# Hybrid decoder layer on one core: token-pass weights rounded two column tiles ahead, and a second instance's token sums cast by halves

## The chip, the cores and the metric

The kernel runs on one core of one Trainium2 chip. A core has a matrix engine (TensorE, PE in the profile, with PEld for its weight loads), a vector engine (VectorE, DVE), a scalar engine (ScalarE, ACT), a general engine (GpSimd, POOL) and a queue engine (SyncE, SP) that issues transfers. Each engine takes its own instructions in a fixed order and waits where an operand is not there yet. The metric is the device time of one execution in microseconds (us); less is better. Every instruction has a line of the kernel in the profile (L1051 is line 1051).

## The reference, cut to what matters

One layer of a hybrid decoder for a prompt of 1024 tokens and 8 single sample tokens, all in 32-bit floats. The 1032 token columns (NT) run through the same weights.

```
h    = rmsnorm(x, norm1_w);  proj = h @ w_in          # 1024 -> 6672 columns
o_a  = gated linear recurrence (8 heads), gated rmsnorm
y    = Mamba-2 mixer (16 heads), gated rmsnorm
x    = x + concat(o_a, y) @ w_out                      # 2048 -> 1024
h    = rmsnorm(x, norm2_w)
gate, val = split(h @ w_up)                            # 1024 -> 2 * 2816
gate = causal_conv(gate, width 3)
x    = x + (silu(gate) * val) @ w_down                 # 2816 -> 1024
y_prompt, y_sample = rmsnorm(x, final_norm_w)
```

The recurrent states and the convolution rows are returned too. The change lies in `concat(o_a, y) @ w_out`, in the second rmsnorm, and in the first two of 22 steps of `h @ w_up`.

## The kernel before, in words

**Precision.** A product of 32-bit values is made from three matmuls on a rounded type (fp32r): each operand is split into a high part (a cast on ACT) and a low part (operand minus high part, on DVE), and PE adds high times high, low times high and high times low. So every weight tile costs an ACT cast, then a DVE subtraction, before PE can use it.

**Jobs.** The first half of the kernel is a list of jobs (`jobs`, L212), each with a load and a run that yields after every matmul. `step` (L255) runs one matmul; `tick` (L239) counts down pieces of other work that `after(n, work)` (L227) put n matmuls ahead, and `spread` (L246) issues a generator piece by piece. PE's order is exactly the written one. On ACT, DVE, POOL and SP a planner orders the instructions by the place at which the program issues them, but by its own cost model it lets a later one pass if the earlier one is not ready; `issue_after(ins)` forbids that an instruction passes `ins`.

**The output projection** is a row of `out_job`s (L1095) over eight column tiles m of 128 columns each:

- a0..a7 and b0..b7: the second and the first 1024 rows of `w_out`, token half 0
- c0..c7: second 1024 rows, token half 1, both quarters of 258 tokens in one job, 48 matmuls
- d00..d07: first 1024 rows, the first quarter of token half 1 only, 24 matmuls each
- d17 down to d10: the same rows, second quarter, 24 matmuls each. The weights of tiles 4 to 7 are kept from the first pass (`wkept`); tiles 3 to 0 are loaded and rounded anew.

A `Weight` (L1034) starts a 512 KB transfer into one of two raw buffers (`ws`); `round` (L1042) casts (L1050) and subtracts (L1051) into a slot pair `wh`, `wl`. The raw buffer is free for the next transfer when the subtraction has ended. Slot pairs come from `wpool` (two) or from `tmp` (two; only tiles 4 and 5 use them). `step` calls `load_ahead` with a depth of 3 jobs and has the next job's weights rounded 1 matmul (24-matmul jobs) or 10 matmuls into the current job. Inside `round` the cast is put behind `mark` (`behind`, L1029): the last square of a finished tile. When a tile's matmuls end, DVE adds the result to x (L1125), SP writes it out (L1135), ACT squares it (L1138, L1141) and POOL adds the square to the row sums (L1142).

**The norm and the token sums.** Tokens go through the up projection in two instances i = 0, 1 (token halves), each of two quarters. `set_norm(i, c)` (L1231) sums the squares over partitions by two matmuls with ones (`n2ms`), and ACT and DVE make the reciprocal root. `set_of(i)` (L1240) scales the tokens (`norm`, L1254) and makes seven operands p1 to p7 (a Strassen-like scheme of seven products in place of eight): p1, p2, p4 are blocks of the tokens themselves, p5, p6, p7, p3 are sums and differences of blocks. `comb` (L1270) makes a sum in two pieces of 516 elements; `put` (L1264, L1265) casts on ACT and subtracts on DVE, for a sum in one piece of 1032. For i = 1, p5 comes from sa = b1 - b2 (DVE), p6 from sa - a1, p7 from sb = a1 - b1 (POOL), p3 from the next sa + a2, one in the place of the other.

**The up projection** (`ups`) runs 22 steps j. A step has 14 products of 12 matmuls: in step 0 all seven of instance 0 and then all seven of instance 1, in the order p1, p2, p4, p5, p6, p7, p3; later steps alternate the instances. `up_split(j, n)` (L1342) casts two weight parts of a step (L1351) and subtracts (L1352). The parts of step 1 are issued in step 0 after the sixth, tenth and fourteenth product. The results of p2, p4, p5, p6 go to four PSUM banks (`ub`), those of p1, p7, p3 to three others (`ua`); DVE and ACT empty them (L1374 to L1409), and `up_close` ends a step with the convolution and SiLU.

**Driving order around the change**: after d07, `set_norm(1, 0)` is put 20 matmuls ahead and ten pieces of `set_of(1)` (those that need only the first quarter) one per 10 matmuls from the 40th; `up_split(0, n)` follow in d13, d11, d10; in step 0, `set_norm(1, 1)` stands after 44 matmuls, and the other pieces of `set_of(1)` follow from the 46th, one per matmul.

Of the kernel before, what the change touches and what calls it, by code (L numbers as in the profile page):

```python
# [9 lines left out]
F32 = mybir.dt.float32  # L10
# [3 lines left out]
ALU = mybir.AluOpType  # L14
# [37 lines left out]
def hybrid_layer(  # L52
# [156 lines left out]

    jobs, loaded, done, later, ahead = [], {}, set(), [], {}  # L212
    at = [0, None]

    def load_ahead(i, n):
# [11 lines left out]
    def after(n, work):  # L227

        item = [n, work]
        later.append(item)  # L230
        return item
# [23 lines left out]
    def step(last):  # L255
        tick()
        if at[1] is None:
            name, load, run = jobs[at[0]]
            nxt = jobs[at[0] + 1][0] if at[0] + 1 < len(jobs) else None
            load_ahead(at[0], 3 if nxt in ahead or name in ahead else 2)  # L260
            if nxt in ahead:
                early, n = ahead[nxt]
                after(n, lambda part=loaded[at[0] + 1]: early(part))
            at[1] = run(loaded[at[0]]) if load is not None else run()
        if next(at[1], None) is None:
            done.add(jobs[at[0]][0])
            at[0] += 1
            at[1] = None
            if last not in done:
                step(last)  # L270
# [821 lines left out]

    wkept, summed = {}, [None, set()]

    def out_job(name, r0, hf, m, cols=(0, 1), begin=None, keep=False):  # L1095
        first, last = r0 == 8, r0 == 0

        def load():
            w = wkept.pop(m, None) or Weight(r0, m)
            if keep:  # L1100
                wkept[m] = w
            return w, residual_load(m, hf) if first else None

        def early(loads):
            loads[0].round(tmp if keep and m in (4, 5) else wpool)

        def run(loads):
            w, res = loads
            early(loads)
            if begin is not None:  # L1110
                begin()
            hi, lo = mixes[r0, hf]
            if first:
                if m % 2 == 0:
                    xpair[hf][m // 2] = tl("big", "x1")[:, :NT].rearrange("p (i t) -> p i t", i=2)
                xh[hf][m] = xpair[hf][m // 2][:, m % 2, :]
            for c in cols:
                cs, ts_ = slice(c * QW, (c + 1) * QW), slice((2 * hf + c) * QW, (2 * hf + c + 1) * QW)
                ps = psmm.tile([P, 512], F32, tag="mm", name=nm("mm"))[:, :QW]
                yield from steps(w.parts, 0, P, hi, lo, cs, ps)  # L1120
                x_ = xh[hf][m][:, cs]
                if first:
                    mark[0] = A.copy(x_, ps)
                else:
                    V.tensor_tensor(x_, x_, ps, op=ALU.add)  # L1125
                    final(m, x_, ts_)
                yield True
            if first:
                spread(residual(xh[hf][m], hf, *res), 8)
        job(name, load, run)  # L1130
        ahead[name] = early, 10 if len(cols) == 2 else 1

    def final(m, x_, ts_):

# [60 lines left out]
    for m in range(KT):  # L1195
        out_job(f"b{m}", 0, 0, m, begin={0: open_b}.get(m))
    for m in range(KT):
        out_job(f"c{m}", 8, 1, m, begin={0: open_c}.get(m))
    for m in range(KT):
        out_job(f"d0{m}", 0, 1, m, (0,), {0: lambda: split_rest(0, 1)}.get(m), m > 3)  # L1200
    for m in reversed(range(KT)):
        out_job(f"d1{m}", 0, 1, m, (1,))

    with tc.manual_schedule(engines={mybir.EngineType.PE}):
        finish("x3")
# [29 lines left out]
        mm(ps[:, :QW], ones, rst[:, cs])  # L1235
        rstd_of(rst[:, cs], tl("us", "nt"), ps[:, :QW], DM)

    usets = [{}, {}]

    def set_of(i):  # L1240

        ts_ = slice(2 * i * QW, 2 * (i + 1) * QW)
        xp = [t.rearrange("p i (c t) -> p i c t", c=2) for t in xpair[i]]

        def block(h1, c):
            return [xp[2 * h1 + q][:, :, c, :] for q in range(2)]

        a1, b1, a2, b2 = block(0, 0), block(0, 1), block(1, 0), block(1, 1)

        def norm(h1, cols=slice(0, MID)):  # L1250
            rs = rst[:, ts_][:, cols]
            for m in range(4 * h1, 4 * h1 + 4):
                x_ = xh[i][m][:, cols]
                V.scalar_tensor_tensor(x_, x_, col("n2", m), rs, op0=ALU.mult, op1=ALU.mult)  # L1254
                yield

        def put(name, src, tag):
            hi, lo = tl(tag, "uh", F32R), tl(tag, "ul", F32R)
            hq, lq = quads(hi[:, :NT]), quads(lo[:, :NT])
            usets[i][name] = hq, lq  # L1260
            n = 4 // len(src)
            for q, t in enumerate(src):
                rows = slice(q * n, (q + 1) * n)
                A.copy(hq[:, rows], t)  # L1264
                V.tensor_tensor(lq[:, rows], t, hq[:, rows].bitcast(F32), op=ALU.subtract)  # L1265
                yield

        def comb(t, eng, x_, y_, op):
            for q in range(2):
                eng.tensor_tensor(t[:, 2 * q:2 * q + 2], x_[q], y_[q], op=op)  # L1270
                yield

        def two(t):
            return [t[:, 0:2], t[:, 2:4]]

        c0, c1 = slice(0, QW), slice(QW, MID)
        if i == 0:
            yield from norm(0)
            yield from norm(1)
            yield from put("p2", a2, "big")  # L1280
            yield from put("p4", b2, "e")
        else:
            yield from norm(1, c0)
            yield from put("p2", a2, "big")
            yield from norm(0, c0)
            yield from put("p1", a1, "hT")
            yield from norm(1, c1)
            yield from put("p4", b2, "hT")
            yield from norm(0, c1)
        sa, sb = (quads(tl("x5", "sm")[:, :NT]) for _ in range(2))  # L1290
        yield from comb(sa, V, b1, b2, ALU.subtract)
        yield from comb(sb, G, a1, b1, ALU.subtract)
        if i == 0:
            while "c7" not in done:
                yield
            yield from put("p1", a1, "hT")
        yield from put("p5", [sa], "hT")
        yield from comb(sa, V, two(sa), a1, ALU.subtract)
        yield from put("p6", [sa], "hT")
        yield from put("p7", [sb], "big" if i else "hT")  # L1300
        yield from comb(sa, V, two(sa), a2, ALU.add)
        yield from put("p3", [sa], "big")

# [38 lines left out]
    def up_split(j, n):  # L1342
# [5 lines left out]
        lo = pool.tile([P, KT * P], F32R, tag="wl", bufs=2, name=nm("wl"))  # L1348
        for i, name in enumerate(order[2 * n:2 * n + 2]):
            cs = slice(i * 512, (i + 1) * 512)  # L1350
            A.copy(hi[:, cs], sums[name])  # L1351
            V.tensor_tensor(lo[:, cs], sums[name], hi[:, cs].bitcast(F32), op=ALU.subtract)  # L1352
            ops_[name] = [t[:, cs].rearrange("p (k m) -> p k m", m=P) for t in (hi, lo)]

# [88 lines left out]
    with tc.manual_schedule(engines={mybir.EngineType.PE}):  # L1443
# [21 lines left out]
        up_split(0, 3)  # L1465
        for _ in early:
            pass
        after(44, lambda: set_norm(1, 1))
        after(46, lambda: spread(second, 1))
        for _ in ups(0, [(name, i) for i in range(2) for name in FIRST]):  # L1470
            tick()
        for j in range(1, FT):
# [124 lines left out]
```

## Time and profile before

| | |
|---|---|
| median of 3 runs | 1792.68 us (1789.44 to 1794.56) |
| profiled execution | 1790.33 us, span 1788.6 us, granted TensorE clock 0.995 |
| PE busy | 1742.4 us, 97% of the span |
| PEld busy | 1684.7 us, 94% |
| DVE busy | 1111.1 us, 62% |
| ACT busy | 797.0 us, 45% |
| POOL busy | 398.2 us, 22% |
| DMA | 105 GB/s mean |

The times in the profile's views count from the start of the span. In a row of the chain of waits the first number is the start, the second the length, both in us, and "x48" is the number of instructions. In a timeline row the same two numbers lead, and the idle time before the row stands in brackets with what ended it. In a table of windows each engine has its busy time and, in brackets, the number of its instructions; PEclk is the granted share of the matrix engine's full clock.

### The profile page before, as it was taken

To read this page: it belongs to the slowest core of one execution; us is meant where nothing else is said; L and a number is where in the kernel's file an instruction comes from. 1 tells how busy PE (TensorE), PEld (TensorE's weight loads), DVE (VectorE), ACT (ScalarE), POOL (GpSimd) and SP (SyncE) were. 2 spreads that over 40 slices of the span, in tenths; PEclk is the share of its full clock that TensorE was granted. 3 is DMA by queue.
4 is the path that set the end of the run, shared out by engine and by line. 5 is a ranking of instruction groups with operands and counts; after the bars stand their busy time and mean duration, and the time that the engine had idled before them with its cause. 6 is when DMAs were issued, how large, how long until landed. Compare 5 with 4: busy or idle time off the path is not lost.

```text
span 1788.6 us, 38536 instructions
## 1 busy us (share of the span) xinstructions
PE 1742.4 (97%) x16223; PEld 1684.7 (94%) x16223; DVE 1111.1 (62%) x1946; ACT 797.0 (45%) x1410; POOL 398.2 (22%) x411
## 2 busy tenths in 40 slices
PE   7999899999999999999999998999999999999998
PEld 7998798999999999999999898999999999999997
DVE  4657967566555554556657668666666666545545
ACT  6477688454544444354344444333433344111114
POOL 1103331110110110111011134454445542000002
PEclk9999999999999999999999998999999999999999
DMA  5135634553222221224466341222222225422212
GB/s 154 36 99 154 171 101 136 170 156 99 72 77 63 73 84 43 81 79 133 144 201 190 113 118 56 87 72 72 84 95 72 72 77 209 143 86 94 96 60 96
DMA packets 240547, 188.66 MB, mean 105 GB/s; under 512 B 13356, under 2 KB 213590, under 8 KB 240358
## 3 DMA queue, kind: packets, MB, share of 16 engines
q1 hardware_dynamic: 240086, 186.11, 34.2%
q8 instruction: 127, 2.08, 0.5%
q14 instruction: 46, 0.38, 0.1%
q0 software_dynamic: 288, 0.10, 0.0%
HBM read 147.84 MB, written 38.52 MB: 104 GB/s over the span
## 4 chain that ended last, share of the span: by engine, by line
PE 46%; DVE 3%; ACT 1%; DMA 1%; issue 0%; DVEq 0%; POOL 0%; ACTq 0%
PE ub L94 14%; PE dn L94 13%; PE ua L94 10%; PE mm L94 7%; DMA ws<-in_w_out_dram 1%; DVE ul L1265 1%; DVE x L1254 0%; DVE wl L1051 0%; DVE sm L1270 0%; PE fin L1552 0%; PE xtp L809 0%; DVE wl L1352 0%; ACT ot L1554 0%; ACT uh L1264 0%; PE l L1491 0%
## 5 line engine op out<-in xcount | busy, mean ns | idle before, releaser
L94 PE MATMUL mm<-hh,wh 128*128 128x344 f32 x1248 | 406.2, 326 | 1.2 <-ACT sz L691 1.2
L94 PE MATMUL mm<-hl,wh 128*128 128x344 f32 x1248 | 403.9, 324 | 0.0
L94 PE MATMUL mm<-hh,wl 128*128 128x344 f32 x1248 | 402.5, 323 | 0.0
L94 PEld LDWEIGHTS mm<-hh,wh 128*128 128x128 f32 x1248 | 234.5, 188 | 4.5 <-ACT sz L691 1.5
L94 PEld LDWEIGHTS mm<-hl,wh 128*128 128x128 f32 x1248 | 234.6, 188 | 2.5 <-issue 0.9
L94 PEld LDWEIGHTS mm<-hh,wl 128*128 128x128 f32 x1248 | 234.8, 188 | 2.2 <-issue 1.0
L94 PE MATMUL ub<-uh,wh 128*128 128x258 f32 x704 | 200.4, 285 | 2.8 <-ACT uh L1264 2.8
L94 PE MATMUL ub<-ul,wh 128*128 128x258 f32 x704 | 200.6, 285 | 2.3 <-DVE ul L1265 2.3
L94 PE MATMUL ub<-uh,wl 128*128 128x258 f32 x704 | 200.0, 284 | 0.0
L94 PE MATMUL mm<-mx,wh 128*128 128x258 f32 x1024 | 191.2, 286 | 2.4 <-DVE mx L1067 1.3
L94 PE MATMUL dn<-ah,wh 128*128 128x256 f32 (+1 forms) x640 | 181.1, 283 | 1.2 <-DVE x L1527 1.2
L94 PE MATMUL dn<-ah,wl 128*128 128x256 f32 (+1 forms) x640 | 180.4, 282 | 0.1
L94 PE MATMUL dn<-al,wh 128*128 128x256 f32 (+1 forms) x640 | 180.3, 282 | 0.0
L189 ACT CAST wh<-ws 128x1024 fp32r<-128x1024 f32 x72 | 75.4, 1048 | 206.7 <-PE dn L94 135.8
L94 PEld LDWEIGHTS mm<-mx,wh 128*128 128x128 f32 x1024 | 158.5, 189 | 3.9 <-DVE mx L1067 1.8
L94 PE MATMUL mm<-mx,wl 128*128 128x258 f32 x512 | 145.9, 285 | 3.9 <-DVE wl L1051 3.8
L94 PE MATMUL ua<-ul,wh 128*128 128x258 f32 x528 | 149.4, 283 | 0.0
L94 PE MATMUL ua<-uh,wh 128*128 128x258 f32 x528 | 149.3, 283 | 0.0
L94 PE MATMUL ua<-uh,wl 128*128 128x258 f32 x528 | 149.2, 283 | 0.0
L94 PEld LDWEIGHTS ub<-uh,wh 128*128 128x128 f32 x704 | 133.8, 190 | 3.4 <-ACT uh L1264 3.3
L94 PEld LDWEIGHTS ub<-ul,wh 128*128 128x128 f32 x704 | 134.2, 191 | 2.8 <-DVE ul L1265 2.8
L94 PEld LDWEIGHTS ub<-uh,wl 128*128 128x128 f32 x704 | 134.3, 191 | 0.0
(332 smaller groups left out, 3739.1 us busy)
## 6 DMA issues: line engine op xcount, KB each, us to landing
ws<-in_w_in_dram SPq DMA_DIRECT2D x52, 512.0 KB
ws<-in_w_up_dram SPq DMA_DIRECT2D x44, 512.0 KB
ws<-in_w_out_dram SPq DMA_DIRECT2D x36, 512.0 KB
act_d<-val SPq DMA_DIRECT2D x22, 516.0 KB
al<-act_d SPq DMA_DIRECT2D x22, 516.0 KB
ws<-in_w_down_dram SPq DMA_DIRECT2D x22, 512.0 KB
mx<-mix_d SPq DMA_DIRECT2D x32, 258.0 KB
csb<-cs_d SPq DMA_DIRECT2D x32, 256.0 KB
```

The source lines that it names most:

```text
L94: PE.matmul(out, lhsT, rhs, start=start, stop=stop)
L189: A.copy(wh[:, :n], ws[:, :n])
L1265: V.tensor_tensor(lq[:, rows], t, hq[:, rows].bitcast(F32), op=ALU.subtract)
```

## The change

Three edits, all in order and place of work; no matmul is added or removed.

1. The weights of a d job are rounded two jobs ahead instead of one (`lead`), with four slot pairs (`pool`: tiles 0, 1, 4, 5 in `tmp`, 2, 3, 6, 7 in `wpool`; the reloaded tiles 3 to 0 in `wpool`). d00 is rounded in c6, d01 in c7. d11 and d10 keep a lead of one. Jobs are loaded deeper ahead (`depth`: 4 from c7 on, up to 6 at d17).
2. In step 0 `set_norm(1, 1)` stands after 22 matmuls, and the rest of `set_of(1)` starts at the 24th. In `set_of(1)` POOL's sb is issued first, and p5, p6 and p3 are made by `comb_put`: each half is added and cast at once, and the two halves' subtractions follow.
3. The casts of step 1's weight parts are put behind the last cast of `comb_put` (`setmark`).

```diff
-            nxt = jobs[at[0] + 1][0] if at[0] + 1 < len(jobs) else None
-            load_ahead(at[0], 3 if nxt in ahead or name in ahead else 2)
-            if nxt in ahead:
-                early, n = ahead[nxt]
-                after(n, lambda part=loaded[at[0] + 1]: early(part))
+            load_ahead(at[0], depths.get(at[0], 3 if at[0] in at_jobs else 2))
+            for i, (j, early) in enumerate(at_jobs.get(at[0], ())):
+                after((1 if name[0] == "d" else 10) + 12 * i, lambda part=loaded[j], early=early: early(part))
...
-            loads[0].round(tmp if keep and m in (4, 5) else wpool)
+            loads[0].round(tmp if pool == "t" else wpool)
...
-        ahead[name] = early, 10 if len(cols) == 2 else 1
+        at_jobs.setdefault(len(jobs) - 1 - lead, []).append((len(jobs) - 1, early))
+        depths[len(jobs) - 1] = depth
...
-        out_job(f"c{m}", 8, 1, m, begin={0: open_c}.get(m))
+        out_job(f"c{m}", 8, 1, m, begin={0: open_c}.get(m), depth=3 if m < 7 else 4)
...
-        out_job(f"d0{m}", 0, 1, m, (0,), {0: lambda: split_rest(0, 1)}.get(m), m > 3)
+        out_job(f"d0{m}", 0, 1, m, (0,), {0: lambda: split_rest(0, 1)}.get(m), m > 3, "ttwwttww"[m], 2, 4)
...
-        out_job(f"d1{m}", 0, 1, m, (1,))
+        out_job(f"d1{m}", 0, 1, m, (1,), pool="wwwwttww"[m], lead=2 if m > 1 else 1, depth=(2, 3, 3, 4, 4, 4, 5, 6)[m])
...
+        def comb_put(name, tag, t, x_, y_, op):
+            hi, lo = tl(tag, "uh", F32R), tl(tag, "ul", F32R)
+            hq, lq = quads(hi[:, :NT]), quads(lo[:, :NT])
+            usets[i][name] = hq, lq
+            half_ = [slice(0, 2), slice(2, 4)]
+            for q, rows in enumerate(half_):
+                V.tensor_tensor(t[:, rows], x_[q], y_[q], op=op)
+                setmark[0] = A.copy(hq[:, rows], t[:, rows])
+                yield
+            for rows in half_:
+                V.tensor_tensor(lq[:, rows], t[:, rows], hq[:, rows].bitcast(F32), op=ALU.subtract)
+            yield
...
+        if i:
+            yield from comb(sb, G, a1, b1, ALU.subtract)
+            yield from comb_put("p5", "hT", sa, b1, b2, ALU.subtract)
+            yield from comb_put("p6", "hT", sa, two(sa), a1, ALU.subtract)
+            yield from put("p7", [sb], "big")
+            yield from comb_put("p3", "big", sa, two(sa), a2, ALU.add)
+            return
...
-            A.copy(hi[:, cs], sums[name])
+            if j == 1:
+                with tc.issue_after(setmark[0].ins):
+                    A.copy(hi[:, cs], sums[name])
+            else:
+                A.copy(hi[:, cs], sums[name])
...
-        after(44, lambda: set_norm(1, 1))
-        after(46, lambda: spread(second, 1))
+        after(22, lambda: set_norm(1, 1))
+        after(24, lambda: spread(second, 1))
```

More of the change, by code (lines that the diff above doesn't have):

```diff
@@ L208, in hybrid_layer @@
     chunks = [slice(c * CH, (c + 1) * CH) for c in range(NCH)]
-    jobs, loaded, done, later, ahead = [], {}, set(), [], {}
+    jobs, loaded, done, later, at_jobs, depths = [], {}, set(), [], {}, {}
     at = [0, None]
@@ L1093, in hybrid_layer, with out_job @@
     wkept, summed = {}, [None, set()]
-    def out_job(name, r0, hf, m, cols=(0, 1), begin=None, keep=False):
+    def out_job(name, r0, hf, m, cols=(0, 1), begin=None, keep=False, pool="w", lead=1, depth=3):
         first, last = r0 == 8, r0 == 0
@@ L1236, in set_norm @@
         rstd_of(rst[:, cs], tl("us", "nt"), ps[:, :QW], DM)
-    usets = [{}, {}]
+    usets, setmark = [{}, {}], [None]
     def set_of(i):
@@ L1290, in set_of @@
         sa, sb = (quads(tl("x5", "sm")[:, :NT]) for _ in range(2))
+        if i:
[5 more added lines that the diff above has]
+            return
         yield from comb(sa, V, b1, b2, ALU.subtract)
         yield from comb(sb, G, a1, b1, ALU.subtract)
[L1293 to L1296, printed above, removed]
+        while "c7" not in done:
+            yield
+        yield from put("p1", a1, "hT")
         yield from put("p5", [sa], "hT")
@@ L1299, in set_of @@
         yield from put("p6", [sa], "hT")
-        yield from put("p7", [sb], "big" if i else "hT")
+        yield from put("p7", [sb], "hT")
         yield from comb(sa, V, two(sa), a2, ALU.add)
```

## The prediction

> **What bounds the kernel now.** I read the page's busy times first, then the waits of PE around the change, the chain of waits there, and last the timelines and groups of ACT, DVE, POOL and SP. The page:
>
> ```profile
> PE 1742.4 (97%) x16223; PEld 1684.7 (94%) x16223; DVE 1111.1 (62%) x1946; ACT 797.0 (45%) x1410; POOL 398.2 (22%) x411
> ```
>
> PE sets the time. An edit of order can only win back time in which PE stands still or runs slowly. Waits of PE from 1000 to 1095 us:
>
> ```profile
> PE mm L94 <- DVE wl L1051: 3.8, 5, 1.4
> PE ub L94 <- ACT uh L1264: 2.8, 2, 1.7
> PE ub L94 <- DVE ul L1265: 2.3, 2, 1.4
> PE mm L94 <- ACT wh L1050: 0.9, 2, 0.7
> ```
>
> Both places of the change are here: the d jobs wait for rounded weights (3.8 + 0.9 us), step 0 for token sums (2.8 + 2.3 us). Waits are not the whole loss, so I count it from the chain of waits:
>
> ```profile
> 994.23 5.97 PE mm L94 x48
> 1000.20 0.44 PE xtp L809 x4
> ...
> 1019.19 5.65 DMA ws<-in_w_out_dram
> ...
> 1027.19 4.13 DMA ws<-in_w_out_dram
> ...
> 1061.88 1.43 PE ua L94 x12
> 1063.31 3.85 PE ub L94 x32
> 1067.16 0.45 PE n2ms L94 x2
> ...
> 1088.25 6.32 PE ua L94 x48
> 1094.57 5.77 PE ub L94 x48
> ```
>
> **d jobs.** An unhindered 258-column matmul takes 5.97/48 = 0.124 us, a tile of 24 takes 2.99. From 994.23 (start of c6) to 1061.88 (end of d10) lie 67.65 us. They hold 2 x 48 matmuls of c6 and c7 and 16 x 24 of the d jobs, 480 x 0.1244 = 59.7, the transposes after c6 and c7 (0.44 and a small one, 0.6 each) and `n2ms` of 0.45: 61.4. So 6.2 us are lost, none of it in c6. **Step 0.** From 1061.88 to 1094.57 lie 32.69 us with 14 x 12 matmuls of step 0 and 24 of step 1: 192 x 0.120 (5.77/48) + 0.45 = 23.5. Lost: 9.2 us, of which 5.1 are waits. The windows show where most of the rest went, and what DVE does meanwhile:
>
> ```profile
> 1068.10:1089.70 21.60, 16.50 (x105) 15.49 (x105) 21.29 (x33) 8.37 (x14) 6.12 (x5) 0.76 0.00 1
> 1076.00:1079.20 3.20, 1.10 (x7) 0.68 (x6) 3.03 (x5) 1.89 (x3) 1.61 (x3) 1.00 0.00 0
> 1079.20:1089.40 10.20, 7.20 (x30) 6.61 (x31) 10.20 (x14) 4.84 (x8) 1.53 (x1) 0.50 0.00 1
> ```
>
> The columns are stretch, length, then busy time of PE, PEld, DVE, ACT, POOL, and the granted clock. PE was busy for 1.10 of 3.20 us, and for the next 10.2 us its clock was 0.50: the waits cost some 4 us more in a slow clock. And DVE is busy for 21.29 of 21.60 us: here it is DVE, not PE, that sets the pace. Recoverable in all: 6.2 + 9.2 = 15.4 us.
>
> **Edit 1, weights two tiles ahead.** It moves one cast (1.03 to 1.06 us on ACT) and one subtraction per tile ahead by a tile; it adds none, and the count of transfers stays (eight for the first pass, four for the second). The subtractions before, of d01 to d07:
>
> ```profile
> L1051 DVE TENSOR_TENSOR wl<-ws,wh x7: 1211/1225/1727, 1008.2 to 1032.5; 128x1024 fp32r<-128x1024 f32 x7
> ```
>
> That is one per 24.3/6 = 4.1 us where PE could take one per 2.99. If the lead only shifts each of these times to the next tile, the time now kept for d01 serves d02, and so on. Unhindered, d0m starts at 994.23 + 2 x (5.97 + 0.6) + 2.99 m, that is 1007.4 + 2.99 m. The rows that decide:
>
> ```profile
> 1014.18 1.22 DVE L1051 TENSOR_TENSOR wl<-ws,wh 128x1024 fp32r<-128x1024 f32 x1
> ...
> 1025.94 1.23 DVE L1051 TENSOR_TENSOR wl<-ws,wh 128x1024 fp32r<-128x1024 f32 x1 [3.27 <-ACT wh L1050]
> 1027.09 0.41 DVE L1125 TENSOR_TENSOR x<-x,mm 128x258 f32<-128x258 f32 x1
> 1028.92 1.23 DVE L1051 TENSOR_TENSOR wl<-ws,wh 128x1024 fp32r<-128x1024 f32 x1 [1.42 <-ACT wh L1050]
> ```
>
> The one that ends at 1015.4 (d02 now, then d03) is 1.0 us early for d03 at 1016.4; the one that ends at 1027.2 (then d06) is 1.9 late for 1025.3; the one at 1030.2 (then d07) is 1.9 late for 1028.3, the same lateness and not a further one. So at fixed times 1.9 us would be left of what d0 loses. The times are not fixed: a cast waits behind the square of an earlier tile, which waits for DVE's addition (L1125, queued behind the subtraction above), and PE will end that tile sooner. Against that stands the raw buffer: cast 1.05, subtraction 1.23 and transfer 4.13 to 5.65 us (chain) make 6.4 to 7.9 us per two tiles where PE takes 5.98, so 0.2 to 1.0 us are lost per tile once the lead is used up. I take 1.2 left in d0 (0 to 3), and 0.5 in d1, whose last two tiles keep a lead of one. **Gain 4.5 us, from 2.5 to 5.7.** Cast and subtraction of d00 and d01 now fall into c6 and c7, where PE runs its 48 matmuls in 5.97 us without a wait; without that cover they would cost a 1.2 us subtraction each. What SP must pass is a transfer issued one job sooner that waits for its buffer; behind it stand only the write-outs of x, for which no engine waits soon.
>
> **Edit 2, step 0.** `n2ms` moves from 44 matmuls in to 22: 22 x 0.120 = 2.65 us sooner, and everything that hangs on it (root, norms, sums) with it. It needs the last row sum on POOL:
>
> ```profile
> 1063.29 0.64 POOL L1142 TENSOR_TENSOR n2r<-n2r,n2sq 128x258 f32<-128x258 f32 x1 [2.09 <-ACT n2sq L1141]
> ```
>
> That ends 2.05 us after PE's step 0 began; the new place is at 2.65, so 0.6 us of room; if DVE is late there, all of PE waits for it, by some tenths. The sums of DVE from 1068 to 1090, by group:
>
> ```profile
> L1270 DVE TENSOR_TENSOR sm<-sm,x 128x516 f32<-128x516 f32 x4 | 2.6, 685 | 0.0
> L1270 DVE TENSOR_TENSOR sm<-x,x 128x516 f32<-128x516 f32 x2 | 2.2, 1138 | 0.0
> ```
>
> A subtraction of a half works on 516 elements like these pieces: some 0.66 us as they follow each other (2.6/4), two 1.3, a whole one 1.23 (row below): +0.1 for each of p5, p6, p3, together 0.3 us, an estimate. The first two sums cost 1138 ns a piece against 685 for the later four; POOL runs its own two pieces of sb in that stretch:
>
> ```profile
> 1075.23 1.49 POOL L1270 TENSOR_TENSOR sm<-x 128x516 f32<-128x516 f32 x1 [0.36 <-DVE x L1254]
> ```
>
> The change puts sb's issue first, so this collision stays, at 0.9 us for the two pieces, and I take no gain from it. The Trainium skill (SBUF — State Buffer, Who interferes with whom) says that a DVE instruction with two SBUF inputs and a GpSimd instruction that reads SBUF exclude each other, and whoever issues second blocks fully. By that rule POOL going first would cost DVE up to the whole 1.49 us per piece and the sum would be some 2 us worse; the trace shows 0.45 a piece, and I go by it.
>
> **Edit 3, step 1's weights behind the sums.** The same stretch for the low weight parts alone (PE and PEld on matmuls that use them, then DVE), and the end of the last token sum:
>
> ```profile
> 1068.10:1089.70 21.60, 11.02 (x35) 7.97 (x35) 3.18 (x4) 0.76 0.00 1
> ```
>
> ```profile
> 1088.46 1.22 DVE L1265 TENSOR_TENSOR ul<-sm,uh 128x1032 fp32r<-128x1032 f32 x1
> ```
>
> Four subtractions, 3.2 us of DVE, leave the stretch ahead of that sum. So p3's operand, complete at 1089.7 (27.8 us into step 0), is complete 2.65 + 3.2 - 0.3 = 5.5 us sooner, 22.3 us in. PE would reach p3 of instance 1 after 156 matmuls, 156 x 0.120 + 0.45 = 19.2 us in. **3.1 us of the 9.2 stay lost, gain 6.1 us**, if no wait is long enough to slow the clock; 0 is left if DVE's emptying of PSUM falls into gaps, 6.5 if the clock slows (by what stays of the 4 us above): 2.7 to 9.2. The postponed weights are then late next: their cast and subtraction (0.6 + 0.7 us) for step 1's p1 come right behind p3's operand, while PE works 12 matmuls on p3 (1.44 us): no wait, and 1.3 us for each part if that cover is gone.
>
> The Trainium skill (TensorE: Matmul & The Clock Gate, HAM oscillation) puts the drop of the clock at idle gaps of over about 3.4 us. Here the longest wait was 1.70 us and the clock still fell, so the trace disagrees if the rule is read as one gap, and agrees if it means a window that is mostly idle. By the single-gap reading no wait left here could slow the clock, and the sum would keep its 6.1 us for certain.
>
> **Sum.** 4.5 + 6.1 = 10.6 us from the profiled execution's 1790.33: 1779.7. That execution is 2.35 us under the median of the runs, 1792.68, so I expect a median of **1782.0 us**.
>
> **Rivals.**
>
> *Emptied too late (B).* Products p2, p4, p5, p6 share four PSUM banks. The addition that empties p6 of instance 0 (L1378) ran between the sums of p5 and their subtraction, in a gap that the whole cast on ACT left:
>
> ```profile
> 1077.20 0.41 DVE L1378 TENSOR_TENSOR us<-us,ub 128x258 f32<-128x258 f32 x1
> ```
>
> Cast by halves leaves hardly a gap, and the sums are now listed 22 matmuls further ahead of this addition. If it falls behind p3's operand, p5 of instance 1 starts about 21 us in and not at 14.9: 6 us of standstill, then a clock of 0.50 for 10.2 us, 5.1 more. 11.1 us lost against 9.2 before, so the sum is 4.5 - 1.9 = 2.6 us: 1790.1. Against it: the cast ends a moment after DVE's second sum, so a small gap remains.
>
> *No gain in the d jobs (C).* DVE stays packed with `set_of(0)`'s sums behind c7 and the raw buffers stay two, so rounding runs at 4.1 us per tile and the lead is used up at once: only the 6.1 us of step 0 remain: 1786.6.
>
> *Second step starved, slower (D).* The postponed subtractions meet the end of step 0 on DVE, and the planner lets later work pass, as here, where a weight part issued later (L1352) went before the d13 subtraction:
>
> ```profile
> 1047.01 1.28 DVE L1352 TENSOR_TENSOR wl<-ws,wh 128x512 fp32r<-128x512 f32 x2
> 1048.22 1.21 DVE L1051 TENSOR_TENSOR wl<-ws,wh 128x1024 fp32r<-128x1024 f32 x1
> ...
> 1094.75 2.65 DVE L358 SCALAR_TENSOR_TENSOR fcv<-fext,vcol,fcv 128x1048 f32<-128x1048 f32 x2
> ...
> 1099.96 2.21 DVE L1425 TENSOR_TENSOR val<-val,fext 128x1032 f32<-128x1032 f32 x1 [1.90 <-ACT fext L1424]
> ```
>
> If the six additions of instance 1 (6 x 0.41 = 2.5 us), the convolution (2.65), the 2.6 us until the product starts (SiLU on ACT, 1097.4 to 1099.96) and the product (2.21) come before step 1's first subtraction, it ends 10.0 + 0.7 us after 22.3, and PE, ready at 23.7, stands for 9 us; with 5.1 for the clock 14 us, which eats 10.6 and 3.4 more: 1796. It turns slower once that wait with its slow clock passes 10.6 us. Against it: the parts are issued before the convolution.
>
> *It does not do what it says (E).* The planner ends in the same order on DVE, which is full either way: 1792.
>
> **How the numbers follow.** Forecast 0.62, B 0.15, C 0.12, D 0.06, E 0.05. The forecast's own range is 1777.8 to 1787.5 (gains of 14.9 to 5.2 by the bounds above). Down to 1776 and up to 1790.5 it takes in C and most of B. A run-to-run spread of 0.3% (5.4 us) is what can be told from no change, so faster means under 1787.3: 0.60 of the forecast, 0.07 of C, 0.03 of B, 0.70. Slower: D and a little of B and E, 0.08. Same: 0.22.
>
> **What would show it.** In the profile of the changed kernel: PE's waits for L1051 and L1050 at 1 to 2 us and not 4.7; `n2ms` 2.65 us into step 0; DVE's L1352 of step 1 behind p3's last L1265; PE's waits for `ub` at 3 us, and no stretch of half clock near 1075. Wrong: a wait of PE for L1378 (B), for L1352 in step 1 (D), or unchanged waits for L1051 (C).

## The result and the profile after

| | before | after |
|---|---|---|
| median | 1794.56 us (7 runs, 1789.44 to 1796.49) | 1788.01 us (7 runs, 1784.51 to 1789.63) |
| profiled execution | 1790.33 us, span 1788.6 | 1789.03 us, span 1787.3 |
| the same kernels timed again | 1793.77 us (15 runs) | 1785.60 us (7 runs) |

The ratio after to before is 0.9966 with an interval of 0.9952 to 0.9981, and 0.9954 (0.9940 to 0.9969) the second time. The kernel is faster by 0.34 to 0.46%, 6.6 and 8.2 us, where 0.6% (10.6 us) was forecast. The first timing stays above the 1787.3 us under which the forecast called it faster.

The two profiled executions differ by 1.3 us only, and that would mislead: in the profile of before, c6 starts at 994.23 us, in that of after at 998.24, after work that the change does not touch: up to there PE, DVE, ACT and POOL run the same instructions in the same order in both. So I compare the two stretches of the prediction. **D** runs from c6 to step 0, **U** from step 0 to the first p6 product of step 1. Chain of waits of after:

```profile
998.24 5.97 PE mm L94 x48
...
1019.45 5.90 DMA ws<-in_w_out_dram
...
1062.02 1.45 PE ua L94 x12
...
1091.18 1.71 PE ua L94 x12
1092.88 5.78 PE ub L94 x48
```

D is 1062.02 - 998.24 = 63.78 us (67.65 before), U is 1092.88 - 1062.02 = 30.86 us (32.69 before). The change gained 3.9 us in the d jobs, where 4.5 were forecast, and 1.8 us in step 0, where 6.1 were. In the second profile of after (from 998.57 to 1062.11 and to 1092.29) they are 63.54 and 30.18: 4.1 and 2.5 us. The miss lies in step 0.

The waits of PE from 1000 to 1100 us, after:

```profile
PE ub L94 <- DVE fext L1424: 1.6, 1, 1.6
PE mm L94 <- DVE wl L1049: 1.5, 2, 0.8
PE mm L94 <- ACT wh L1048: 0.9, 2, 0.6
PE ub L94 <- DVE ul L1285: 0.9, 2, 0.7
PE ub L94 <- DVE us L1400: 0.5, 1, 0.5
PE ua L94 <- ACT us L1396: 0.5, 1, 0.5
```

L1049 and L1048 are the rounding of the d jobs (L1051 and L1050 before): 2.4 us in place of 4.7. L1285 is a token remainder. New are L1424 and L1400, for which PE waits 2.1 us: they are the emptyings of the PSUM banks of p4 and p6 by DVE. L1396 is an emptying by ACT. The windows of after (columns as in the prediction) say what came behind:

```profile
1077.86:1081.27 3.41, 1.75 (x12) 1.57 (x13) 3.41 (x8) 2.15 (x4) 1.10 (x2) 1.00 0.01 2
1081.27:1088.10 6.83, 6.13 (x28) 5.83 (x28) 6.83 (x11) 4.44 (x10) 1.65 (x1) 0.50 0.00 0
```

PE was busy 1.75 of 3.41 us, and its clock then was 0.50 for 6.83 us (10.24 before). The last place to read is what moved next to what. First POOL and DVE of before, around the root of the second norm, then the same of after:

```profile
1063.88 1.29 POOL L1332 TENSOR_TENSOR wt<-ws 128x512 f32<-128x512 f32 x1
...
1067.74 1.29 POOL L1332 TENSOR_TENSOR wt<-wt,ws 128x512 f32<-128x512 f32 x1
```

```profile
1068.14 0.43 DVE L666 SCALAR_TENSOR_TENSOR nt<-n2ms,n2r 128x258 f32<-128x258 f32 x1 [2.85 <-ACT n2r L665]
1068.60 0.72 DVE L667 SCALAR_TENSOR_TENSOR nt<-nt,n2r 128x258 f32<-128x258 f32 x1
1069.35 0.43 DVE L668 SCALAR_TENSOR_TENSOR n2r<-nt,n2r 128x258 f32<-128x258 f32 x1
1069.81 1.69 DVE L1254 SCALAR_TENSOR_TENSOR x<-x,vcol,n2r 128x258 f32<-128x258 f32 x4
```

```profile
1064.16 1.28 POOL L1350 TENSOR_TENSOR wt<-ws 128x512 f32<-128x512 f32 x1
1065.52 1.30 POOL L1350 TENSOR_TENSOR wt<-wt,ws 128x512 f32<-128x512 f32 x1
1066.77 1.48 POOL L1350 TENSOR_TENSOR wt<-ws,ws 128x512 f32<-128x512 f32 x1
1068.21 1.47 POOL L1350 TENSOR_TENSOR wt<-wt,ws 128x512 f32<-128x512 f32 x1
```

```profile
1065.78 0.42 DVE L664 SCALAR_TENSOR_TENSOR nt<-n2ms,n2r 128x258 f32<-128x258 f32 x1
1066.24 0.86 DVE L665 SCALAR_TENSOR_TENSOR nt<-nt,n2r 128x258 f32<-128x258 f32 x1
1067.14 1.40 DVE L666 SCALAR_TENSOR_TENSOR n2r<-nt,n2r 128x258 f32<-128x258 f32 x1
1068.57 2.59 DVE L1253 SCALAR_TENSOR_TENSOR x<-x,vcol,n2r 128x258 f32<-128x258 f32 x4
...
1076.86 0.41 DVE L1400 TENSOR_TENSOR us<-us,ub 128x258 f32<-128x258 f32 x1
...
1080.56 0.41 DVE L1424 TENSOR_TENSOR fext<-us,ub 128x258 f32<-128x258 f32 x1
```

POOL makes four sums of step 1's weights (`up_sums`). Before, they ran from 1063.88 to 1069.03 us, and for 2.85 of these 5.15 us DVE stood idle ahead of the root. The change moved the root into them: the last two operations of the root and the first four norms took 0.86 + 1.40 + 2.59 = 4.85 us and not 0.72 + 0.43 + 1.69 = 2.84. And the emptying of p6 (L1400) and p4 (L1424) of instance 0 stands between the token sums on DVE: p6 was complete 7.8 us into step 0 (1069.7) and p7, which p4's emptying needs, at 9.3 (1071.1), so they are emptied 7 to 9 us late.

### The profile page after: what moved, and what is told of

It is laid out like the page before. It is cut to its first block, busy times and chain, and to the rows that moved or that the text cites. A ratio compares the mean times of both kernels' runs of the same rounds, so it can differ in the third digit from the quotient of the medians.

```text
span 1787.3 us, 38542 instructions
## 1 busy us (share of the span) xinstructions
PE 1742.0 (97%) x16223; PEld 1685.8 (94%) x16223; DVE 1112.5 (62%) x1949; ACT 797.4 (45%) x1413; POOL 397.8 (22%) x411
## 4 chain that ended last, share of the span: by engine, by line
PE 45%; DVE 3%; ACT 1%; DMA 1%; issue 0%; DVEq 0%; POOL 0%; ACTq 0%
PE ub L94 14%; PE dn L94 13%; PE ua L94 10%; PE mm L94 7%; DMA ws<-in_w_out_dram 1%; DVE x L1253 1%; DVE wl L1049 0%; DVE ul L1264 0%; PE fin L1574 0%; PE xtp L807 0%; ACT ot L1576 0%; ACT uh L1263 0%; ACT wh L1048 0%; DVE ul L1285 0%; DVE sm L1281 0%
```

## The experiments

All marks of all kernels, one profile each, are in the table. **R** is the time from step 0's first matmul to the end of p3's last remainder of instance 1 (in after 1061.86 to 1086.23; the matmul's own record starts 0.16 us ahead of its piece of the chain). R marks how far DVE's queue has come; it is not itself what PE waits for in after, where p3's first matmul of instance 1 starts at 1087.35, 1.1 us behind R. "Waits" are PE's waits within U, "rest" is U - 23.5 (PE's unhindered work by the prediction) - waits; "half clock" is the time at 0.50 within U. Medians are given where a kernel was timed more than once (e3 and e4 took 1791.08 and 1790.60 us, one time each). All diffs are against after.

| kernel | D | R | U | waits | rest | half clock | median, ratio to before |
|---|---|---|---|---|---|---|---|
| before | 67.65 | 27.97 | 32.69 | 5.10 | 4.09 | 10.24 | |
| e1_weights | 63.17 | 28.05 | 33.23 | 5.18 | 4.55 | 10.24 | 1790.41, 0.9973 (0.9960 to 0.9985) |
| e2_step0 | 67.45 | 24.02 | 29.77 | 3.75 | 2.52 | 3.41 | 1790.42, 0.9976 (0.9965 to 0.9987) |
| e3_no_behind | 63.41 | 24.66 | 30.37 | 4.08 | 2.79 | 3.41 | |
| e4_norm44 | 63.60 | 25.30 | 31.67 | 3.82 | 4.35 | 6.83 | |
| after | 63.78 | 24.37 | 30.86 | 3.45 | 3.91 | 6.83 | 1788.01, 0.9966 (0.9952 to 0.9981) |
| after_again | 63.54 | 24.32 | 30.18 | 4.04 | 2.64 | 3.41 | 1785.60, 0.9954 (0.9940 to 0.9969) |
| e7_sums_late | 63.57 | 26.06 | 31.35 | 4.86 | 2.99 | 3.41 | 1790.15, 0.9976 (0.9963 to 0.9989) |
| e8_sb_dve | 63.92 | 24.05 | 29.94 | 3.75 | 2.69 | 3.41 | 1789.11, 0.9970 (0.9957 to 0.9983) |
| e10_emptied | 63.31 | 26.11 | 30.78 | 3.48 | 3.80 | 6.83 | 1788.31, 0.9971 (0.9957 to 0.9985) |
| e11_emptied_sums | 63.50 | 29.47 | 33.79 | 7.00 | 3.29 | 6.83 | 1790.88, 0.9982 (0.9973 to 0.9992) |
| e12_sums_last | 63.59 | 22.04 | 27.89 | 3.64 | 0.75 | 0 | 1786.80, 0.9957 (0.9940 to 0.9974) |
| e13_sums_dve | 63.53 | 22.04 | 29.12 | 4.86 | 0.76 | 0 | 1788.12, 0.9967 (0.9954 to 0.9980) |
| e14_three_dve | 63.25 | 22.60 | 28.00 | 3.76 | 0.74 | 0 | 1786.57, 0.9952 (0.9935 to 0.9970) |

D and R repeat to 0.3 us between the two profiles of after. Among kernels that share the part they spread a little more: D from 63.17 to 63.92 in all with edit 1, R from 24.02 to 24.37 in e2 and the two profiles of after, whose step 0 is the same. The rest is 0.75 us without half clock, 2.5 to 3.0 with 3.41 us of it, 3.3 to 4.35 with 6.83, 4.1 to 4.55 with 10.24: a slow clock costs 1.8 to 3.8 us here, and 3.41 against 6.83 us of it is a difference between two runs of one kernel. Medians spread by some 2 us (after alone 1788.01 and 1785.60), so the marks, not the medians, tell these kernels apart.

**Edit 1 alone** (the d jobs' weights two tiles ahead; step 0 as before).

```diff
...
-            yield from comb_put("p5", "hT", sa, b1, b2, ALU.subtract)
...
-                with tc.issue_after(setmark[0].ins):
...
-        after(22, lambda: set_norm(1, 1))
-        after(24, lambda: spread(second, 1))
+        after(44, lambda: set_norm(1, 1))
+        after(46, lambda: spread(second, 1))
```

> The changed kernel with step 0 as before (n2ms after 44 matmuls, whole casts, no cast put behind): only the weights two tiles ahead are left. Measures: D, from the first matmul of c6 to the first of step 0 (67.65 us before, 63.78 in the changed kernel, 61.4 unhindered), and U, from there to the first p6 product of step 1 (32.69 before, 30.86 changed, 23.5 unhindered). Theory 1 (the two parts add up, and the lead won 3.9 us by itself): D 63.8, U 32.7, some 4 us under the kernel before, ratio 0.998. Rival (the two parts disturb each other: DVE work that the lead moves falls into step 0): U over 33.5 or D under 63. Rival C of the prediction (no gain from the lead): D 67.

D fell by 4.48 us, U stayed (33.23, with waits of 5.18). The waits of PE, e1:

```profile
PE ub L94 <- ACT uh L1263: 2.9, 2, 1.8
PE ub L94 <- DVE ul L1264: 2.3, 2, 1.4
PE mm L94 <- DVE wl L1049: 1.5, 2, 0.8
```

The d jobs' part is edit 1's and of the forecast's size; the waits of step 0 are those of before.

**Edits 2 and 3 alone.**

```diff
...
-        out_job(f"d0{m}", 0, 1, m, (0,), {0: lambda: split_rest(0, 1)}.get(m), m > 3, "ttwwttww"[m], 2, 4)
+        out_job(f"d0{m}", 0, 1, m, (0,), {0: lambda: split_rest(0, 1)}.get(m), m > 3, "wwwwttww"[m])
...
-        out_job(f"d1{m}", 0, 1, m, (1,), pool="wwwwttww"[m], lead=2 if m > 1 else 1, depth=(2, 3, 3, 4, 4, 4, 5, 6)[m])
+        out_job(f"d1{m}", 0, 1, m, (1,), pool="wwwwttww"[m])
```

> The changed kernel with the weights of the d jobs rounded one tile ahead in the old slots: only the edits of step 0 are left. Theory 1 (the parts add up, and the edits of step 0 win only 1.8 us because DVE's root and norms now run beside POOL's sums for step 1 and because PE waits for a PSUM bank): D 67.6, U 30.9, 2 us under the kernel before, ratio 0.999. Rival (the lead disturbs step 0; alone its edits win what was forecast): U 26.6, 6 us under.

D is that of before (67.45), U 29.77 and R 24.02: step 0 alone gains 2.9 us, not the 1.8 expected nor the 6 of the rival, with the same wait for L1424 (1.6 us) as after. Alone the two parts gain 4.5 and 2.9 us by the marks, 7.4 in sum; together they gained 5.7 and 6.6 in the two profiles of after. D's spread and the half clock (3.41 us here, 6.83 and 3.41 there) are as large as that difference, so a small hindrance is neither shown nor excluded.

**After without edit 3, and after with the norm at its old place** (44 and 46 in place of 22 and 24).

```diff
-            if j == 1:
-                with tc.issue_after(setmark[0].ins):
-                    A.copy(hi[:, cs], sums[name])
-            else:
-                A.copy(hi[:, cs], sums[name])
+            A.copy(hi[:, cs], sums[name])
```

> The changed kernel without the third edit: step 1's weight casts are not put behind the last token sum. As forecast, this edit takes four subtractions, 3.2 us of DVE, out of the way of the last sum: U 34, D unchanged at 63.8. Rival (postponing costs at the start of step 1 what it wins before): U 30.9 or less.

> The changed kernel with n2ms and the rest of the second token set back at 44 and 46 matmuls. If moving it up won 2.65 us as forecast: U 33.5. Theory 1 (the root and the norms now run beside POOL's four sums for step 1 and take 2 us longer for it: root and first four norms 1.28 + 0.86 + 1.40 + 2.59 us in the place of 1.6 + 1.7): U 31.4, half a us more than the changed kernel's 30.86.

Without edit 3, U is 30.37 and not 34, and R is 24.66 against 24.37 and 24.32: the edit is worth some 0.3 us, no more than the spread of R, and not 3.2. With edit 2 in place only one of step 1's four weight subtractions (L1370) still went ahead of p3's last remainder (L1285), as DVE's timeline without edit 3 shows:

```profile
1086.72 0.68 DVE L1370 TENSOR_TENSOR wl<-ws,wh 128x512 fp32r<-128x512 f32 x1
1087.32 1.29 DVE L1285 TENSOR_TENSOR ul<-sm,uh 128x516 fp32r<-128x516 f32 x2
```

With the norm at its old place, R is 25.30 and U 31.67, near the 31.4 of the first theory: moving the root 2.50 us up gained 0.9 to 1.0 us of R and nothing of the waits (3.82 against 3.45 and 4.04). So R fell from 27.97 to 25.30 by the halves with the casts behind them, and by 0.9 to 1.0 more by the move. No run has the halves without both the move and edit 3, so what the halves do by themselves is not shown.

**POOL's sums later.** Two theories for what ate the move: POOL's sums slow DVE (shared port), or DVE is full to the same point anyway. A third is the bank by itself. In this kernel the sums begin 18.7 us into step 0 and not 2.3, that is 16.4 us later.

```diff
...
-            with tc.issue_after(summed[0].ins):
+            with tc.issue_after(umark[0].ins if j == 1 else summed[0].ins):
...
-        G.tensor_tensor(self.u2, self.f, self.u2, op=ALU.subtract)
+        umark[0] = G.tensor_tensor(self.u2, self.f, self.u2, op=ALU.subtract)
```

> The kernel after, but POOL's four weight sums of step 1 stand behind POOL's two operations of product p7 of the first instance (some 12 us later), so that they no longer run beside DVE's root and norms. U is the time from step 0's first matmul to step 1's first p6 product: 30.86 us after, 32.69 before. Theory 'shared port': in after, the root and the four norms took 0.86, 1.40 and 2.59 us beside the sums, where before had 0.72, 0.43 and 1.68 without them; they win back about 2 us, p4's and p5's operands are ready that much sooner, and U falls to 28.5-29.5 (run about 1786.5). Rival 'full DVE': the sums only collide with the subtractions that follow, DVE stays full to the same point; U 30.4-31.4. Rival 'bank': the root and norms are faster, but the 1.59 us wait for p4's bank stays as its emptying is queued behind the combinations; U falls by under 1.

DVE and POOL in that kernel, timelines:

```profile
1066.41 0.43 DVE L665 SCALAR_TENSOR_TENSOR nt<-nt,n2r 128x258 f32<-128x258 f32 x1
1066.87 0.43 DVE L666 SCALAR_TENSOR_TENSOR n2r<-nt,n2r 128x258 f32<-128x258 f32 x1
1067.33 1.68 DVE L1253 SCALAR_TENSOR_TENSOR x<-x,vcol,n2r 128x258 f32<-128x258 f32 x4
...
1081.24 3.47 DVE L1281 TENSOR_TENSOR sm<-sm,x 128x516 f32<-128x516 f32 x2
1084.64 0.41 DVE L1431 TENSOR_TENSOR val<-us,ua 128x258 f32<-128x258 f32 x1
1084.97 3.12 DVE L1285 TENSOR_TENSOR ul<-sm,uh 128x516 fp32r<-128x516 f32 x2
```

```profile
1080.73 1.73 POOL L1350 TENSOR_TENSOR wt<-ws 128x512 f32<-128x512 f32 x1
...
1085.81 1.73 POOL L1350 TENSOR_TENSOR wt<-wt,ws 128x512 f32<-128x512 f32 x1
```

The first half of the theory held: without the sums the root and norms took 0.43 + 0.43 + 1.68 us, and everything behind them came 2.3 us sooner (R's chain up to p5's last remainder: 14.30 us against 16.62). The second half I had wrong: I expected U at 28.5 to 29.5, and it was 31.35, in the range of the rival "full DVE", and as that rival said the sums collided with what followed. The sums, 6.81 us on POOL at their new place, made two operations of DVE last 3.47 us and two 3.12, where two last 1.29: 4.0 us lost, on p3's own operand. The price is not tied to the root; it falls wherever DVE has work with both operands in SBUF. The emptying at 1084.64, with one operand in PSUM, kept its 0.41 us in the middle of a sum. The Trainium skill (SBUF — State Buffer, Who interferes with whom) has just this: an instruction of DVE with two SBUF inputs and a GpSimd instruction that reads SBUF shut each other out. The trace agrees in the main: POOL's sums last 1.62 to 1.73 us, and the four DVE operations beside them 1.43 to 1.78 instead of 0.68. Strictly one after the other, the four pairs would take 4 x (1.28 + 0.65) = 7.7 us, and the sums were through in 6.81.

**sb on DVE.** Takes POOL's two pieces of sb out of the stretch, at the price of two more operations on DVE.

```diff
-            yield from comb(sb, G, a1, b1, ALU.subtract)
+            yield from comb(sb, V, a1, b1, ALU.subtract)
```

> The kernel after, but the two halves of sb (1.28 and 1.49 us on POOL, beside DVE's norms and p5's combination) are computed on DVE. Theory 'shared port': DVE gets two operations of about 0.69 us more, and loses the excess that it has beside POOL (three norms 2.12 us for 1.28, two combinations 2.20 for 1.38: 1.7 us); U 30.3-31.0, no later than after. Rival 'full DVE without contention': DVE simply has 1.4 us more; U 31.8-32.4.

Timeline of DVE, first after, then this kernel:

```profile
1072.69 2.12 DVE L1253 SCALAR_TENSOR_TENSOR x<-x,vcol,n2r 128x258 f32<-128x258 f32 x3
1074.74 2.20 DVE L1281 TENSOR_TENSOR sm<-x,x 128x516 f32<-128x516 f32 x2
```

```profile
1074.32 1.27 DVE L1253 SCALAR_TENSOR_TENSOR x<-x,vcol,n2r 128x258 f32<-128x258 f32 x3
1075.51 1.29 DVE L1269 TENSOR_TENSOR sm<-x 128x516 f32<-128x516 f32 x2
1076.72 1.28 DVE L1281 TENSOR_TENSOR sm<-x,x 128x516 f32<-128x516 f32 x2
```

DVE does 1.29 us more and is done no later (R 24.05 against 24.37 and 24.32; U 29.94, a little under the 30.3 expected at least): POOL's two pieces had cost DVE (2.12 - 1.27) + (2.20 - 1.28) = 1.8 us. What POOL takes off DVE's hands there is no relief at all.

**Emptied first.** The second instance's p4 remainder, its last norms and all behind them wait on DVE for the emptying of p6, p7 and p4 of instance 0. For this the first weight parts of step 1 are issued after the eighth product of step 0 and no longer after the sixth.

```diff
...
             yield from norm(1, c1)
-            yield from put("p4", b2, "hT")
-            yield from norm(0, c1)
+            while fmark[0] is None:
+                yield
+            yield from put("p4", b2, "hT", fmark[0])
+            yield from norm(0, c1, fmark[0])
...
-            if n in (5, 9, 13) and j + 1 < FT:
-                up_split(j + 1, (5, 9, 13).index(n))
+            if n in (FIVE[j > 0], 9, 13) and j + 1 < FT:
+                up_split(j + 1, (FIVE[j > 0], 9, 13).index(n))
```

> The kernel after, but the second instance's p4 subtraction, its last four norms and all behind them are queued on DVE behind the three emptyings of the first instance's p6, p7 and p4 (1.2 us of DVE that move ahead of 8 us of work). Theory 'bank': the waits of 0.54 and 1.59 us for the banks that p6 and p4 hold are gone and nothing takes their place; U 28.7-29.4. Rival 'full DVE': what is behind comes 1.2 us later and PE waits that much more for p4's and p5's remainders (0.16 and 0.70 in after); U 30.2-31.6.

> Both edits: the sums late and the emptyings first. If the port and the bank are separate causes that add, U is 26.8-28.3 and the run about 1784.5; if DVE is full to the same point whatever the order, U stays at 30-31. The half-clock windows are to be counted: one window of 3.41 us costs 1.7 us of PE time, and if it is the waits that bring them, both vanish (after: 6.83 us at half clock).

Waits of PE with the emptying first, then with the sums late as well:

```profile
PE ub L94 <- DVE ul L1287: 2.0, 3, 1.4
...
PE ub L94 <- ACT uh L1284: 1.5, 1, 1.5
```

```profile
PE ub L94 <- ACT uh L1284: 5.3, 1, 5.3
```

The waits for these banks are gone, and PE waits the same 3.5 us for the operands (ACT's cast of p5 waits for DVE's sum): R is 26.11, U 30.78, as the rival "full DVE" had it. So here the bank wait is a mark of a late DVE, not a cause of its own. "Separate causes that add" is wrong, and U at 30 to 31 whatever the order is wrong too: with both edits the sums ran beside the last four norms, which took 5.75 us where four take 1.68, and U rose to 33.79.

**No sums beside DVE until p3's last remainder.** A copy of 16 columns of that remainder stands ahead of them on POOL.

```diff
+            gate = G.tensor_copy(t7[:, 0:16], usets[1]["p3"][1][:, 3, 242:258].bitcast(F32))
+            with tc.issue_after(gate.ins):
+                G.tensor_tensor(t7, v1, v2, op=ALU.add)
```

> The kernel after, but POOL's four sums of step 1 wait until the last remainder of the second instance's p3 is formed: a copy of 16 columns of that remainder stands ahead of them on POOL, and what it writes the first sum overwrites. R is the time from step 0's first matmul to the end of that last remainder: 24.37 us after, 24.0-24.7 in the kernels with the same step 0, 26.06 with the sums 12 us later, where DVE lost 4.0 us to them. Theory 'DVE is the bound from the root on and what POOL takes beside it is added': with nothing of the sums in that stretch R is 22.0-22.4, which is the forecast's 22.3; but the sums then run beside step 1's own subtractions and p6's weights are ready some 5 us behind R, so U is 27.0-28.5. Rival 'PE or a bank sets R': R stays at 23.5-24.5.

R is 22.04 us (1083.02 - 1060.98): the sums beside the root and norms cost 2.3 us of DVE in after, and without them the forecast's 22.3 is met. PE's waits for the banks of p6 and p4 fall from 2.1 to 0.5 us, and the clock stays full. PE's waits:

```profile
PE ua L94 <- DVE us L1415: 1.8, 1, 1.8
...
PE ub L94 <- DVE fext L1431: 0.5, 1, 0.5
```

U is 27.89, not 26.6, because the sums are now late themselves: PE waits 1.85 us for L1415 (an emptying that stood on DVE behind a weight remainder, whose cast on ACT had waited for POOL's sum), and 1.1 us more just behind U, so that of the 3.0 us by which U is shorter than in after 1.9 are left. Up to R, PE's waits fell from 2.99 to 1.79 us; over all of U they are as long as in after (3.64 against 3.45 and 4.04), and what U gained is the half clock that did not come. DVE is what sets R, and what POOL reads beside it is added to R.

**Two, then three of the four sums on DVE** in its idle time ahead of the root, the others on POOL behind p3's last remainder. For this step 1's weights are loaded after the first product of step 0, not after the third.

```diff
...
-        rstd_of(rst[:, cs], tl("us", "nt"), ps[:, :QW], DM)
...
+        with tc.issue_after(rmark[0].ins) if rmark[0] else nullcontext():
+            rstd_of(rst[:, cs], tl("us", "nt"), ps[:, :QW], DM)
...
-        p7 = add("p7", v1, v2)
-        p6 = add("p6", p7, g1)
...
+            V.tensor_tensor(p7, v1, v2, op=ALU.add)
+            rmark[0] = V.tensor_tensor(p6, p7, g1, op=ALU.add)
...
-            if n == 2 and j + 1 < FT:
+            if n == (2 if j else 0) and j + 1 < FT:
                 up_load(j + 1)
+                if j == 0:
+                    up_sums(1)
...
```

> The kernel after, but step 1's sums of p7 and p6 are made by DVE in the 1.4 us in which it is idle ahead of the root (between p3's weight remainder and the first emptying), and p5's and p4's by POOL behind the second instance's last remainder, as in the run with all sums last. Theory 'what POOL takes beside DVE is added': R 22.0-22.6, p6's weights are no longer late, U is R plus 4.35 us (three products of PE), up to 1.7 more where a half-clock window lies behind R: 26.4-28.3, 2.5-4.5 below after; the run about 1784.5 where after is 1788.0. Rival: DVE's idle time is not there when the weights land, the root starts later by what the two sums take (1.4 us): R 23.5-24, U 28-30.

> As the run with two sums on DVE, but p5's sum is made by DVE too, and POOL keeps only p4's, behind the second instance's last remainder, so that ScalarE's cast of p5's weights no longer waits for POOL ahead of its copy of p1 (the wait of 3.06 us on PE in that run). If DVE is the bound from the root on, the third sum (0.68 us) runs past DVE's idle time and delays the root: R 22.5-22.9 (22.04 with two or none); the copy of p1 is on time, and U is R plus 4.4 to 5.0: 27.0-27.9, 1.7 at most more with a half-clock window; 2.5-3.5 below the kernel after, the run at 1783-1786. Rival: another wait takes the place of the copy's (p4's cast, queued ahead of it, waits for POOL's last sum): U 28.5-29.5.

With two on DVE, R was 22.04 as expected, U 29.12 and not 26.4 to 28.3. ACT's rows and PE's wait tell why:

```profile
1085.20 0.62 ACT L1385 CAST wh<-wt 128x512 fp32r<-128x512 f32 x1 [1.20 <-POOL wt L1362]
1086.87 0.62 ACT L1385 CAST wh<-wt 128x512 fp32r<-128x512 f32 x1 [1.05 <-POOL wt L1351]
...
1087.91 0.37 ACT L1410 COPY us<-ua 128x258 f32<-128x258 f32 x1
```

```profile
PE ua L94 <- ACT us L1410: 3.1, 1, 3.1
```

ACT's copy of p1 stood behind two casts that waited for POOL. Without that wait U would have been 26.1, an estimate (29.12 - 3.06). With three sums on DVE the root starts 0.54 us later (R 22.60), the copy's wait is 1.41 us and U 28.00, just above the 27.0 to 27.9 expected; the rival (p4's cast ahead of the copy) had its share. The medians missed too: 1788.12 us with two sums on DVE, where 1784.5 was expected, and 1786.57 with three, where 1783 to 1786 was. The last is a ratio of 0.9952 (0.9935 to 0.9970). It is faster than before; that it beats after (0.9966 and 0.9954) is not shown by the times. U is 2.2 to 2.9 us shorter than in after, but its waits are no shorter (3.76 us): the difference is the half clock, and the last section says how far that is luck.

The kernel after, unchanged, beside these:

> The kernel after, unchanged, to see how far the marks of one profile repeat. D (from c6's first matmul to step 0) 63.4-63.9, R 24.0-24.7, the wait for p4's bank 1.6 us; U 29.7-30.9 with the half-clock windows of 3.41 us coming out as one or two.

All of it came out so (D 63.54, R 24.32, the bank wait 1.6 us, U 30.18 with one window of 3.41 us).

## Why the prediction was wrong, by its own steps

- **Direction right, size too large.** 1782.0 us was forecast, 1788.01 measured, inside the range. Of the 6.0 us, 1.9 are the base: the 1792.68 of three runs was 1794.56 with seven. The other 4.1 are the sum: 10.6 forecast, 6.5 measured.
- **Edit 1: held.** 4.5 forecast; 3.9 and 4.1 in the two profiles of after, 4.5 alone. The waits left are 2.4 us where 1.7 were put; one raw buffer's transfer, 5.90 us in the chain, was a little beyond the 4.13 to 5.65 that I had.
- **Edit 2, the step that failed first: "2.65 us sooner, and everything that hangs on it".** `n2ms` came 2.64 us sooner and the root 2.50, but R only 0.9 to 1.0 (norm at the old place against after). What hangs on the root got slower, as the move set it beside POOL's sums, which had run in DVE's idle 2.85 us. I looked at POOL for the row sum and for sb, and not at what else POOL did at the new time. Taking the sums away gave 2.3 us of R back, and R was 2.1 late against the forecast (24.4 and not 22.3).
- **The weight against the Trainium skill: decided the wrong way.** I took 0.45 us a piece from the trace and not the exclusion that the Trainium skill (SBUF — State Buffer, Who interferes with whom) states. sb cost DVE 1.8 us for two pieces, and the sums 4.0 us where DVE had work throughout. The 0.45 was read from p5's two sums alone (0.9 together): before, only the second of them was slowed, and the other 0.85 us lay on a norm (1.33 us at 1073.82 instead of 0.48). For sb this cost nothing, as before and after pay the same 1.8 us; what it hid is the price of the four weight sums.
- **Edit 3: "four subtractions, 3.2 us of DVE, leave".** They left, but with edit 2 in place three of the four were gone already: edit 3 is worth some 0.3 us, no more than the spread of R. Together, halves and edit 3 made 27.97 into 25.30, that is 2.7 of the forecast 2.9 (3.2 - 0.3). The sum of the two was right, its assignment not: that the number fits is in part luck.
- **"3.1 us of the 9.2 stay lost", if the clock holds: the term that was mis-sized.** In after, U lost 30.86 - 23.5 = 7.4 us: waits 3.45, of about the size forecast but at other places, 0.75 that no wait explains (it stands in the kernels without half clock too), and 3.2 for half clock; 1.9 in the second profile. I had put the clock's part at nothing and kept it for the range. With none of POOL's sums ahead of p3's last remainder there was no half clock in three profiles of three, but not because the waits were all short: see the last section.
- **Rival B** was there in its mechanism, at a third of its price: 2.1 us for banks, not 6. It was not the cause: with the banks emptied first the waits moved to the operands, at the same sum (3.48 us). C did not come (D gained). D did not come: in after PE had no wait for a weight remainder in step 1. E did not come: DVE's order changed.
- **Not settled:** what ends a stretch of half clock. That after had 6.83 us of it in one profile and 3.41 in the other goes with the position of the grid on which it begins (last section).

## What to carry to other kernels

Before a step is moved, list what every engine does at the new time, not only at the old one: work that ran in another engine's idle time is free only as long as that idle time is there, and the move takes it away. Where DVE is the bound, an operation given to POOL with its operands in SBUF can cost DVE as much as doing it itself; put it where DVE is idle or works from PSUM. A wait for a PSUM bank can be a sign of a late queue: emptying it sooner then only moves the wait.

## What the runs showed of the hardware

- DVE and POOL hindered each other at operations with two SBUF operands: with the sums late, a 128x516 operation of DVE (0.68 us) lasted 1.43 to 1.78 us beside them, and POOL's own sum 1.62 to 1.73 instead of 1.28. DVE's operations with one PSUM operand stayed at 0.41 us.
- Half clock came in stretches of 3.41, 6.83 and 10.24 us. The length of a single wait does not decide it in these runs. In the kernel with two sums on DVE, PE stood for 3.06 us and was busy for 0.28 of 3.34, and the clock stayed at 1.00:

```profile
1084.99:1088.33 3.34, 0.28 (x3) 0.07 (x1) 3.20 (x5) 2.03 (x4) 1.85 (x2) 1.00 0.00 0
```

What the traces show instead is a fixed grid. Within each of the 14 profiles the drops to half clock, also those hundreds of us apart, lie whole multiples of 3.413 us from each other (458 of them between 216.28 and 1779.59 us in this kernel). I cut each profile from 20 to 1700 us along its grid. In the stretch just ahead of a drop PE was busy for 0.51 of the time or less (37 drops, all but one at 0.46 or less); every stretch at full clock with less than 0.46 was followed by a drop, and none with more than 0.52 was. The wait of 3.06 us was split between two stretches of the grid, in each of which PE was busy for more than half:

```profile
1083.27:1086.68 3.41, 2.00 (x17) 1.79 (x16) 3.27 (x5) 1.36 (x3) 3.33 (x3) 1.00 0.00 0
1086.68:1090.10 3.42, 1.76 (x14) 1.77 (x15) 3.05 (x8) 1.81 (x4) 1.46 (x3) 1.00 0.11 30
```

Had one stretch held the whole wait, PE would have been busy for about a tenth of it, and by these shares the clock would have dropped: that this kernel kept its clock was luck of the grid's position. With three sums on DVE the emptiest 3.41 us (from 1078.70) had PE busy for 1.10 us, so that was luck too; with all sums last they had 1.56 (from 1083.95), at the edge. The two profiles of after differ in that position too: in one the stretch ahead of the drop held 1.75 us of PE's work, in the other 1.08.

In after, the longest wait was 1.6 us, PE was busy for 1.75 of 3.41, and the clock fell. The Trainium skill (TensorE: Matmul & The Clock Gate, HAM oscillation) speaks of idle gaps over about 3.4 us. The unit of 3.41 us agrees; as a bound for a single gap it is not what these runs show, since shorter waits were followed by a drop.
